# Nineteen reciprocal square roots: one GpSimd power in place of a guess and three Newton steps on VectorE

## The chip, the core and the metric

One NeuronCore of a Trainium2 chip runs one program. The metric is device microseconds of one execution, the median over several runs. Engines go by the profile's names: PE is TensorE, PEld its weight load, DVE VectorE, ACT ScalarE, POOL GpSimd, SP SyncE (it only issues DMAs here). Each engine works through its own list of instructions in order, and a semaphore is what makes one wait for another.

## The reference

Two stacked blocks on 256 tokens of width 1024, in float32. Block 1 normalises the embedding, modulates it by adaLN vectors, runs multi-head latent attention and RWKV7 side by side, a projection, a layer norm, a top-4 router and 32 experts. Block 2 has two layers of feed-forward, mixing (forgetting attention, dilated attention, HGRN2) and feed-forward, and a last norm. Each norm needs 1/sqrt of a few numbers per token:

```python
def layer_norm(x, g, b):
    xf = x.astype(jnp.float32)
    mu = xf.mean(-1, keepdims=True)
    var = jnp.square(xf - mu).mean(-1, keepdims=True)
    return ((xf - mu) * lax.rsqrt(var + LN_EPS) * g + b).astype(x.dtype)

def rms_norm(x, g):
    xf = x.astype(jnp.float32)
    return (xf * lax.rsqrt(jnp.square(xf).mean(-1, keepdims=True) + RMS_EPS) * g).astype(x.dtype)
```

The key of RWKV7 is divided by the norm of each head, and its output is normalised by head; these need the same function.

## The kernel before

The 256 tokens stand on 128 partitions in two halves, so a statistic per token is a tile of 128 x 1 or 128 x 2, and one per token and head of 128 x 8. The kernel is written as Python generators for the streams and is scheduled by a tile framework that simulates a timeline: it decides in which order each engine's list holds the instructions of independent streams. So an edit at one place can move others.

Line numbers here are those of the kernel before. The program in order of time:

- 0 to 262 us, block 1 up to the router. The embedding's norm (`ln_stats`, call at L551, two calls, 128 x 1) gives `xn` (L313), which PE transposes (L318) and L319 copies out as `axT`; `modT` (L591) comes from adaLN matrix-vector products on PE (`matvec`, weights `in_ada_w` against `cb`); L363 and L364 make the modulated input `moT` and its rounded copy, and then PE starts the input projection (L152, operands `w`). L1088 copies a constant, `iota`, which waits for the DMA of the constants `cst`. Attention and two halves `r` and `s` of RWKV7 then run interleaved. Calls: `rk` (L818, 128 x 8, once per half; its result is copied by L820 for a broadcast on PE), `mrs` (L628, 128 x 4), `gn` (L1033, 128 x 8, once per half, used by L1035), `mro` (L738, 128 x 2), `l2` (L563, 128 x 2, ahead of the router; `nb` at L565 follows it).
- 262 to 1231 us, the experts: 384 DMAs of 1 MB of weights.
- 1231 to 1252 us, `moe_end`: the second layer norm of block 1 (`l2` again). `block2_buffers` prepares the first weights of block 2 beside it, by splits of two-part float32 weights: ACT writes the high part (L198), and here POOL the low part (L203, four instructions of 128 x 1024; elsewhere DVE does L203).
- 1252 to 2309 us, block 2: triple matmuls of split operands (L152); `st` (L1538, 128 x 2, once per norm: four feed-forwards, two mixings, one final) and `hg` (L1865, 128 x 8, once per mixing). In a feed-forward and in mixing the norm's factor is wanted when the first products leave PSUM. ACT loads a table of functions whenever the next function is not in the one at hand (ACT_TABLE_LOAD).
- 2309 to 2329 us, `final`: the last norm, whose factor L1899 (DVE) and L1901 (ACT) apply to the output.

All 19 calls go through `rsqrt`, which issues 12 DVE instructions: an affine form or a floor (L179, L181), a bit trick on the integer view (L182), a multiplication by -0.5 (L183), and three Newton steps (L187 twice for n = 2, else L189 and L190, then L191).

Of the kernel before, what the change touches and what calls it, by code (L numbers as in the profile page):

```python
# [10 lines left out]
I32 = mybir.dt.int32  # L11
U32 = mybir.dt.uint32
AF = mybir.ActivationFunctionType
OP = mybir.AluOpType
# [13 lines left out]

BASE_AT, SETUP_AT, REST_AT = 6, 8, 10

PAD = (176, 8, 8, 8)
MAGIC = 12582912.0
PI_CLIP = 3.1415925
TWO_PI = (6.28125, 0.0019350051879882812, 3.0199159819471256e-07)
# [85 lines left out]
class K:  # L120
    def __init__(self, ctx, tc, I, dbg=None):
        self.ctx, self.tc, self.nc, self.I = ctx, tc, tc.nc, I
        self.dbg_ap = dbg or {}
        nc = self.nc
        self.per = ctx.enter_context(tc.tile_pool(name="per", bufs=1))
        self.rings = [ctx.enter_context(tc.tile_pool(name=n, bufs=b)) for n, b in (("ring", RING), ("ring2", RING2))]
        self.ring_i = None
        self.banks(ctx, p=2, r=2, s=2, m=2)
        self.n = 0
        self.plan = PLAN  # L130
        self.pairs = N_EXP // 2


    def t(self, pool, shape, tag, dt=F32, bufs=None):
        self.n += 1
        kw = {} if bufs is None else {"bufs": bufs}
        return pool.tile(shape, dt, tag=tag, name=f"{tag}_{self.n}", **kw)
# [33 lines left out]

    def rsqrt(self, pool, x, n, scale=1.0, eps=0.0, floor=None, tag="rs", eng=None):

        v = eng or self.nc.vector
        xe = self.t(pool, [128, n], tag + "x", bufs=2)
        y = self.t(pool, [128, n], tag + "y", bufs=2)
        u = self.t(pool, [128, n], tag + "u", bufs=2)
        if floor is None:
            v.tensor_scalar(xe, x, scale, eps, op0=OP.mult, op1=OP.add)  # L179
        else:  # L180
            v.tensor_scalar(xe, x, floor, None, op0=OP.max)  # L181
        v.tensor_scalar(y.bitcast(I32), xe.bitcast(I32), -0.5, 1597463007.0, op0=OP.mult, op1=OP.add)  # L182
        v.tensor_scalar(xe, xe, -0.5, None, op0=OP.mult)  # L183
        for _ in range(3):
            if n == 2:
                for c in (slice(0, 1), slice(1, 2)):
                    v.scalar_tensor_tensor(u[:, c], y[:, c], xe[:, c], y[:, c], op0=OP.mult, op1=OP.mult)  # L187
            else:
                v.tensor_tensor(u, y, y, op=OP.mult)  # L189
                v.tensor_tensor(u, u, xe, op=OP.mult)  # L190
            v.scalar_tensor_tensor(y, u, 1.5, y, op0=OP.add, op1=OP.mult)  # L191
        return y

    def split(self, hi, lo, src, hi_eng="s", lo_eng="v"):
# [33 lines left out]
    def load_consts(self):  # L228
        nc, I = self.nc, self.I
        n = C_ARR.shape[1]  # L230
        self.cst = self.t(self.A, [128, n + PAD[2]], "cst")[:, 0:n]
        first = self.t(self.per, [128, 129 + PAD[0]], "ident")[:, 0:129]
        nc.sync.dma_start(first, I["cst"][:, 0:129])
# [857 lines left out]
    def router(self, Ro, plg, mv, rs, space):  # L1091
# [46 lines left out]
        V.tensor_copy(self.over, most)  # L1138
        self.hgate = t(per, [128, 64 + PAD[1]], "hgate")[:, 0:64].rearrange("p (a e) -> p a e", a=2)
        V.tensor_scalar(self.hgate, gate, 0.5, None, op0=OP.mult)  # L1140
# [303 lines left out]
    def b2_setup(self, B):  # L1444
# [49 lines left out]
        for l in range(2):  # L1494
            nc.gpsimd.dma_start(self.ffw[:, l], I["w_in_2"][l, :, 768:772].rearrange("(k p) c -> p k c", p=128))
        self.rst2 = t(B, [128, T + PAD[3]], "rst2")[:, 0:T]
        nc.gpsimd.memset(self.rst2, 1.0)
# [451 lines left out]
```

## Time and profile before

| what | value |
|---|---|
| three runs | 2331.54, 2335.95, 2336.69 us, median 2335.95 |
| the profiled execution: time, span from first to last instruction | 2330.31 us, 2328.6 us |
| PE, PEld busy | 2264.0 us (97%), 1648.8 us (71%) |
| DVE busy | 1176.1 us (51%), 2237 instructions |
| ACT, POOL busy | 719.1 us (31%), 160.0 us (7%) |
| mean granted TensorE clock | 0.979 of full speed |

Busy shares are means over stages with different limits: the experts' stage follows the DMAs, block 2 follows PE, and the stage up to 262 us changes hands from one stretch to the next. A low share of DVE or POOL over the whole therefore does not say whether one of their instructions is waited for. That is read at each of the 19 places from the timeline, whose columns are start, length, engine and line, operation, and, in brackets, how long the engine was idle before and what released it.

### The profile page before, as it was taken

To read this page: it belongs to the slowest core of one execution; us is meant where nothing else is said; L and a number is where in the kernel's file an instruction comes from. 1 tells how busy PE (TensorE), PEld (TensorE's weight loads), DVE (VectorE), ACT (ScalarE), POOL (GpSimd) and SP (SyncE) were. 2 spreads that over 40 slices of the span, in tenths; PEclk is the share of its full clock that TensorE was granted. 3 is DMA by queue.
4 is the path that set the end of the run, shared out by engine and by line. 5 is a ranking of instruction groups with operands and counts; after the bars stand their busy time and mean duration, and the time that the engine had idled before them with its cause. 6 is when DMAs were issued, how large, how long until landed. Compare 5 with 4: busy or idle time off the path is not lost.

```text
span 2328.6 us, 37824 instructions
## 1 busy us (share of the span) xinstructions
PE 2264.0 (97%) x15957; PEld 1648.8 (71%) x15957; DVE 1176.1 (51%) x2237; ACT 719.1 (31%) x1187; POOL 160.0 (7%) x189
## 2 busy tenths in 40 slices
PE   7999999999999989999998999999999999999998
PEld 6777734444344433344436999989999999999998
DVE  5768322222142321222216666987657656997664
ACT  4333111001000110000004445654444445555443
POOL 3320000000000000000002001021001000121000
PEclk9889999999999999999998999999999999999999
DMA  8625999999999998999996555425555554535550
GB/s 325 188 75 188 339 409 404 411 412 412 419 415 420 420 420 348 412 407 411 410 414 245 187 184 168 156 76 181 181 181 181 182 182 148 180 107 180 182 182 19
DMA packets 275968, 626.47 MB, mean 269 GB/s; under 512 B 14576, under 2 KB 160368, under 8 KB 275760
## 3 DMA queue, kind: packets, MB, share of 16 engines
q1 hardware_dynamic: 274240, 621.38, 71.4%
q8 instruction: 128, 2.10, 0.4%
q0 software_dynamic: 1264, 2.08, 0.3%
q10 hardware_dynamic: 288, 0.52, 0.1%
q14 instruction: 48, 0.39, 0.0%
HBM read 622.89 MB, written 1.05 MB: 268 GB/s over the span
## 4 chain that ended last, share of the span: by engine, by line
PE 55%; DMA 3%; DVE 3%; issue 1%; ACT 1%; DVEq 0%; ACTq 0%
PE p L152 17%; PE s L152 17%; PE m L152 13%; PE r L152 8%; DMA w<-in_exp_w_dram 3%; DVE w L203 1%; PE r L1303 0%; PE s L1748 0%; DVE w L1510 0%; ACT w L1509 0%; PE r L1304 0%; DVE xx L1545 0%; DVE AT L1814 0%; DVE w L1804 0%; DVE z L1784 0%
## 5 line engine op out<-in xcount | busy, mean ns | idle before, releaser
L203 DVE TENSOR_TENSOR w<-w,w 128x1024 fp32r<-128x1024 f32 (+2 forms) x360 | 440.0, 1230 | 267.9 <-ACT w L198 267.8
L198 ACT CAST w<-w 128x1024 fp32r<-128x1024 f32 (+2 forms) x364 | 374.7, 1040 | 454.1 <-PE m L152 255.1
L152 PE MATMUL s<-w,w 128*128 128x256 f32 (+1 forms) x2392 | 306.3, 280 | 4.4 <-ACT w L198 4.4
L152 PE MATMUL m<-w,w 128*128 128x256 f32 (+1 forms) x2240 | 303.5, 285 | 3.7 <-DVE w L203 2.0
L152 PEld LDWEIGHTS s<-w,w 128*128 128x128 f32 (+1 forms) x2392 | 287.2, 189 | 6.7 <-ACT w L198 4.5
L152 PEld LDWEIGHTS m<-w,w 128*128 128x128 f32 (+1 forms) x2240 | 282.8, 192 | 6.9 <-DVE w L203 2.9
L152 PE MATMUL p<-w,xg 128*64 128x512 f32 x1024 | 269.3, 601 | 10.8 <-PEq L1365 5.6
L152 PE MATMUL s<-w,xg 128*64 128x512 f32 x1024 | 263.0, 597 | 0.0
L152 PE MATMUL p<-w,w 128*128 128x256 f32 x1728 | 228.8, 288 | 0.0
L152 PEld LDWEIGHTS p<-w,w 128*128 128x128 f32 x1728 | 214.5, 192 | 7.7 <-issue 6.0
L152 PEld LDWEIGHTS p<-w,xg 128*64 128x64 f32 x1024 | 89.9, 137 | 159.9 <-issue 135.8
L152 PEld LDWEIGHTS s<-w,xg 128*64 128x64 f32 x1024 | 90.0, 136 | 146.3 <-issue 134.3
L1207 DVE TENSOR_TENSOR ag<-r,adas 128x512 f32<-128x512 f32 x32 | 22.1, 692 | 306.7 <-PE r L1303 306.5
L1180 ACT ACTIVATE xg<-m,B,A 128x128 f32<-128x128 f32 x62 | 28.4, 457 | 364.4 <-DVE xg L1182 359.3
L152 PE MATMUL p<-w,u 128*64 128x512 f32 x512 | 126.8, 597 | 1.1 <-DMA w<-in_exp_w_dram 1.1
L152 PE MATMUL s<-w,u 128*64 128x512 f32 x512 | 121.9, 596 | 2.6 <-DMA w<-in_exp_w_dram 2.6
L1533 POOL TENSOR_TENSOR w<-w,th 128x256 f32<-128x256 f32 x47 | 40.8, 867 | 846.0 <-PE p L152 544.7
L152 PEld LDWEIGHTS s<-w,u 128*64 128x64 f32 x512 | 44.2, 136 | 73.4 <-issue 64.0
L152 PEld LDWEIGHTS p<-w,u 128*64 128x64 f32 x512 | 45.0, 136 | 70.2 <-issue 63.0
L1182 DVE TENSOR_SCALAR xg<-m,A,B 128x128 f32<-128x128 f32 x62 | 25.4, 410 | 136.8 <-PE m L152 126.9
L152 PEld LDWEIGHTS m<-oh,xx 128*128 128x128 f32 x496 | 59.1, 194 | 27.1 <-issue 24.3
L1299 ACT COPY h<-s 128x512 f32<-128x512 f32 x32 | 18.8, 586 | 192.7 <-PE s L152 192.7
(726 smaller groups left out, 2752.1 us busy)
## 6 DMA issues: line engine op xcount, KB each, us to landing
w<-in_exp_w_dram SPq DMA_DIRECT2D x384, 1024.0 KB, 18.1
w<-in_ffn_w_gate_dram SPq DMA_DIRECT2D x44, 1024.0 KB, 5.2
w<-in_ffn_w_up_dram SPq DMA_DIRECT2D x44, 1024.0 KB, 5.2
w<-in_ffn_w_down_dram SPq DMA_DIRECT2D x44, 1024.0 KB, 4.9
w<-in_w_in_dram SPq DMA_DIRECT2D x29, 1024.0 KB, 5.1
w<-in_ada_w_dram SPq DMA_DIRECT2D x24, 1024.0 KB, 5.5
w<-in_w_out_dram SPq DMA_DIRECT2D x8, 1024.0 KB, 4.9
w<-in_w_in_dram SPq DMA_DIRECT2D x8, 896.0 KB, 9.7
```

Of the source, the lines that this page charges most:

```text
L152: return self.nc.tensor.matmul(out, lhsT, rhs, start=start, stop=stop, skip_group_check=True, **kw)
L198: nc.scalar.copy(hi, src)
L203: (nc.vector if lo_eng == "v" else nc.gpsimd).tensor_tensor(lo, src, hi, op=OP.subtract)
L1180: S.activation(xg[:, d], p[:, j * 128:(j + 1) * 128], AF.Identity, scale=self.A2[:, d:d + 1], bias=self.B2[:, d:d + 1])
L1182: V.tensor_scalar(xg[:, d], p[:, j * 128:(j + 1) * 128], self.A2[:, d:d + 1], self.B2[:, d:d + 1], op0=OP.mult, op1=OP.add)
L1207: V.tensor_tensor(gl, pg, bg, op=OP.add)
L1299: S.copy(h[:, nb * 512:(nb + 1) * 512], hp[nb])
L1533: G.tensor_tensor(q[:, 0], q[:, 0], sq, op=OP.add)
```

## The change

`rsqrt` keeps its first DVE instruction (affine form or floor) and then issues one POOL instruction: the elementwise power of two tensors, with a tile `mhalf` of -0.5 as the exponent. `mhalf` (128 x 8) is set once by a POOL memset at the program's start, and a pad of the memory plan (`PAD`) is eight columns smaller for it. The scratch tile `u` is gone.

```diff
--- before.py
+++ after.py
@@ -28,7 +28,7 @@
 
 BASE_AT, SETUP_AT, REST_AT = 6, 8, 10
 
-PAD = (176, 8, 8, 8)
+PAD = (168, 8, 8, 8)
 MAGIC = 12582912.0
 PI_CLIP = 3.1415925
 TWO_PI = (6.28125, 0.0019350051879882812, 3.0199159819471256e-07)
@@ -127,6 +127,8 @@
         self.ring_i = None
         self.banks(ctx, p=2, r=2, s=2, m=2)
         self.n = 0
+        self.mhalf = self.t(self.per, [128, 8], "mhalf")
+        self.nc.gpsimd.memset(self.mhalf, -0.5)
         self.plan = PLAN
         self.pairs = N_EXP // 2
 
@@ -171,24 +173,14 @@
 
     def rsqrt(self, pool, x, n, scale=1.0, eps=0.0, floor=None, tag="rs", eng=None):
 
-        v = eng or self.nc.vector
+        V, G = self.nc.vector, self.nc.gpsimd
+        y = self.t(pool, [128, n], tag + "y", bufs=2)
         xe = self.t(pool, [128, n], tag + "x", bufs=2)
-        y = self.t(pool, [128, n], tag + "y", bufs=2)
-        u = self.t(pool, [128, n], tag + "u", bufs=2)
-        if floor is None:
-            v.tensor_scalar(xe, x, scale, eps, op0=OP.mult, op1=OP.add)
+        if floor is not None:
+            V.tensor_scalar(xe, x, floor, None, op0=OP.max)
         else:
-            v.tensor_scalar(xe, x, floor, None, op0=OP.max)
-        v.tensor_scalar(y.bitcast(I32), xe.bitcast(I32), -0.5, 1597463007.0, op0=OP.mult, op1=OP.add)
-        v.tensor_scalar(xe, xe, -0.5, None, op0=OP.mult)
-        for _ in range(3):
-            if n == 2:
-                for c in (slice(0, 1), slice(1, 2)):
-                    v.scalar_tensor_tensor(u[:, c], y[:, c], xe[:, c], y[:, c], op0=OP.mult, op1=OP.mult)
-            else:
-                v.tensor_tensor(u, y, y, op=OP.mult)
-                v.tensor_tensor(u, u, xe, op=OP.mult)
-            v.scalar_tensor_tensor(y, u, 1.5, y, op0=OP.add, op1=OP.mult)
+            V.tensor_scalar(xe, x, scale, eps, op0=OP.mult, op1=OP.add)
+        G.tensor_tensor(y, xe, self.mhalf[:, 0:n], op=OP.pow)
         return y
 
     def split(self, hi, lo, src, hi_eng="s", lo_eng="v"):
```

By count: DVE has 11 x 19 = 209 instructions fewer, POOL 19 powers and a memset more. The rows of the lists fall from 2073 to 1884 on DVE and rise from 171 to 191 on POOL. ACT's rise from 1074 to 1079: among them are four table loads, two in each mixing, since the two functions of `fox_masks` (L1694, L1695) now stand apart from L1760. In the rows below the lines of the changed kernel are lower by 8 than those of before (L195 is L203, L812 is L820).

DVE at the program's start, before: `lny` is the result of the embedding's norm, `w_80<-w_79` the normalised embedding, `modT` the adaLN vectors, `iota` the constant.

```order
L313 TENSOR_SCALAR w_80<-w_79,bmv_132,lny_135 128x1024
L191 SCALAR_TENSOR_TENSOR lny_156<-lnu_157,lny_156 128x1
L313 TENSOR_SCALAR w_80<-w_79,bmv_153,lny_156 128x1024
L319 COPY axT_70<-m_177 128x512
L319 COPY axT_70<-m_189 128x512
L591 TENSOR_TENSOR modT_128<-r_245,col_16_106 128x2x2
L357 TENSOR_SCALAR A_50_230<-modT_128 128x2
L358 TENSOR_TENSOR B_51_231<-col_16_106,A_50_230 128x2
L359 TENSOR_TENSOR B_51_231<-B_51_231,modT_128 128x2
L360 TENSOR_TENSOR A_50_230<-A_50_230,col_16_106 128x2
L1088 COPY iota_2687<-cst_88 128x96
L363 TENSOR_SCALAR moT_71<-axT_70,A_50_230,B_51_231 128x256 x2
```

DVE at the same place in the changed kernel:

```order
L295 SCALAR_TENSOR_TENSOR cact_126<-cth_124,col_17_108 128x8
L297 TENSOR_SCALAR cb_128<-cact_126 128x256
L583 TENSOR_TENSOR modT_130<-r_225,col_17_108 128x2x2
L349 TENSOR_SCALAR A_49_210<-modT_130 128x2
L350 TENSOR_TENSOR B_50_211<-col_17_108,A_49_210 128x2
L351 TENSOR_TENSOR B_50_211<-B_50_211,modT_130 128x2
L352 TENSOR_TENSOR A_49_210<-A_49_210,col_17_108 128x2
L1080 COPY iota_2623<-cst_90 128x96
L305 TENSOR_SCALAR w_82<-w_81,bmv_134,lny_136 128x1024
L305 TENSOR_SCALAR w_82<-w_81,bmv_144,lny_146 128x1024
L311 COPY axT_72<-m_157 128x512
L355 TENSOR_SCALAR moT_73<-axT_72,A_49_210,B_50_211 128x256 x2
```

The normalised embedding (L305, was L313) has moved from ahead of `modT` to behind the copy of `iota`, and the first `moT` stands between the two copies of `axT`.

DVE at the RWKV key norms, before, from the last steps of half `r` to the first of half `s`:

```order
L190 TENSOR_TENSOR rkru_948<-rkru_948,rkrx_946 128x8
L191 SCALAR_TENSOR_TENSOR rkry_947<-rkru_948,rkry_947 128x8
L820 COPY w_838<-rkry_947 128x512
L837 SCALAR_TENSOR_TENSOR w_895<-Z_72,col_37_195,w_894 128x256
L181 TENSOR_SCALAR rksx_922<-s_917 128x8
L837 SCALAR_TENSOR_TENSOR w_895<-Z_72,col_37_195,w_894 128x256
L182 TENSOR_SCALAR rksy_923<-rksx_922 128x8
L837 SCALAR_TENSOR_TENSOR w_838<-Z_72,col_37_195,w_837 128x256 x2
L183 TENSOR_SCALAR rksx_922<-rksx_922 128x8
L189 TENSOR_TENSOR rksu_924<-rksy_923 128x8
L190 TENSOR_TENSOR rksu_924<-rksu_924,rksx_922 128x8
L191 SCALAR_TENSOR_TENSOR rksy_923<-rksu_924,rksy_923 128x8
```

The same place in the changed kernel:

```order
L180 TENSOR_SCALAR rkrx_916<-r_910 128x8
L815 TENSOR_SCALAR w_874<-w_873,col_36_175,oka_204 128x256 x2
L834 COPY ebcs_936<-w_874 128x8
L815 TENSOR_SCALAR w_817<-w_816,col_36_175,oka_204 128x256 x2
L812 COPY w_818<-rkry_915 128x512
L180 TENSOR_SCALAR rksx_903<-s_897 128x8
L829 SCALAR_TENSOR_TENSOR w_875<-Z_74,col_36_175,w_874 128x256 x2
L829 SCALAR_TENSOR_TENSOR w_818<-Z_74,col_36_175,w_817 128x256 x2
L823 TENSOR_TENSOR w_817<-w_817,r_938 128x512
L825 TENSOR_TENSOR w_816<-w_817,w_816 128x512
L812 COPY w_875<-rksy_902 128x512
```

The two copies for the broadcast (L812, was L820) have no Newton steps ahead of them any more; that of half `s` stands behind four instructions of L829 and two of other lines.

POOL at the end of the experts, before: four low parts of weights, then the first products of block 2.

```order
L1909 MEMSET w_7768 128x1
L203 TENSOR_TENSOR w_7776<-w_7774,w_7776 128x1024
L203 TENSOR_TENSOR w_7779<-w_7774,w_7779 128x1024
L203 TENSOR_TENSOR w_7784<-w_7782,w_7784 128x1024
L203 TENSOR_TENSOR w_7787<-w_7782,w_7787 128x1024
L1533 TENSOR_TENSOR w_7768<-w_7768,th_7875 128x256
```

And in the changed kernel:

```order
L1901 MEMSET w_7671 128x1
L195 TENSOR_TENSOR w_7679<-w_7677,w_7679 128x1024
L195 TENSOR_TENSOR w_7682<-w_7677,w_7682 128x1024
L183 TENSOR_TENSOR l2y_7704<-l2x_7705,mhalf_67 128x2
L195 TENSOR_TENSOR w_7687<-w_7685,w_7687 128x1024
L195 TENSOR_TENSOR w_7690<-w_7685,w_7690 128x1024
L1525 TENSOR_TENSOR w_7671<-w_7671,th_7767 128x256
```

The power of `l2` stands behind the second low part and ahead of the third.

## Rows read from the trace of the kernel before

**Rows 1.** The page: busy us, share of the span and instructions by engine.

```profile
PE 2264.0 (97%) x15957; PEld 1648.8 (71%) x15957; DVE 1176.1 (51%) x2237; ACT 719.1 (31%) x1187; POOL 160.0 (7%) x189
```

**Rows 2.** Timeline, end of the MoE: start, length, engine line; idle, releaser.

```profile
1235.15 9.26 POOL L203 TENSOR_TENSOR w<-w,w 128x1024 fp32r<-128x1024 f32 x4 [25.72 <-ACT w L198]
...
1239.87 2.26 DVE L182 TENSOR_SCALAR l2y<-l2x 128x2 int32<-128x2 int32 x1
...
1246.20 0.16 DVE L565 SCALAR_TENSOR_TENSOR nb<-bmv,l2y 128x2 f32<-128x2 f32 x1
...
1247.34 0.69 PE L1421 MATMUL p<-ident,w 128*128 128x128 f32 x2 [8.73 <-DVE w L1416]
```

**Rows 3.** Timeline, final norm.

```profile
2320.26 0.16 DVE L179 TENSOR_SCALAR stx<-s 128x2 f32<-128x2 f32 x1 [1.79 <-PE s L152]
...
2322.41 0.16 DVE L191 SCALAR_TENSOR_TENSOR sty<-stu,sty 128x2 f32<-128x2 f32 x1
...
2322.66 0.69 ACT L1901 ACTIVATE w<-p,sty 128x512 f32<-128x512 f32 x1 [3.75 <-DVE sty L191]
```

**Rows 4.** Timeline, router's norm.

```profile
261.45 0.17 DVE L179 TENSOR_SCALAR l2x<-bmv 128x2 f32<-128x2 f32 x1
...
263.82 0.16 DVE L191 SCALAR_TENSOR_TENSOR l2y<-l2u,l2y 128x2 f32<-128x2 f32 x1
```

**Rows 5.** Windows: length, busy (count) by engine, PEclk, DMA share, GB/s.

```profile
95.00:100.00 5.00, 2.14 (x22) 1.62 (x24) 4.83 (x15) 0.79 (x2) 1.43 (x2) 0.84 0.59 184
100.00:135.00 35.00, 35.00 (x448) 26.68 (x442) 20.43 (x52) 4.99 (x11) 8.08 (x6) 0.50 0.29 96
225.00:230.00 5.00, 5.00 (x46) 2.60 (x46) 4.71 (x28) 1.77 (x4) 0.45 (x1) 0.69 0.87 315
260.00:265.00 5.00, 2.54 (x19) 2.26 (x18) 4.75 (x30) 1.54 (x4) 0.00 (x0) 0.72 1.02 419
```

**Rows 6.** Timeline, RWKV key norms: DVE, then PE.

```profile
92.25 0.43 DVE L820 COPY w<-rkry 128x512 f32<-128x512 f32 x1
...
100.68 0.40 DVE L820 COPY w<-rksy 128x512 f32<-128x512 f32 x1
...
99.20 1.94 PE L152 MATMUL p<-w,cb 128*32 128x256 f32 x16 [2.86 <-DVE modT L603]
```

**Rows 7.** ACT group of table loads at L1768; windows of mixing, layer 1.

```profile
L1768 ACT ACT_TABLE_LOAD x2 | 2.6, 1283 | 0.0
...
1475.00:1560.00 85.00, 84.91 (x701) 81.42 (x700) 82.87 (x141) 51.23 (x88) 17.97 (x11) 1.00 0.38 124
1565.00:1570.00 5.00, 3.11 (x20) 2.16 (x18) 3.72 (x24) 2.82 (x10) 0.00 (x0) 0.95 0.00 0
```

**Rows 8.** Groups on POOL, one on DVE: shape, count | busy us, mean ns.

```profile
L878 POOL TENSOR_TENSOR w<-w,cst 128x512 f32<-128x512 f32 x8 | 10.6, 1341 | 32.3 <-PE s L152 15.9 <-ACT w L861 14.3 <-PE r L152 2.0
...
L203 POOL TENSOR_TENSOR w<-w,w 128x1024 fp32r<-128x1024 f32 x4 | 9.3, 2350 | 25.7 <-ACT w L198 25.7
...
L1909 POOL MEMSET w<- 128x1 f32 x5 | 0.5, 99 | 196.8 <-PE p L152 192.4 <-DMA w<-in_exp_w_dram 4.1 <-issue 0.3
...
L203 DVE TENSOR_TENSOR w<-w,w 128x1024 fp32r<-128x1024 f32 x342 | 421.5, 1239 | 252.5 <-ACT w L198 252.3
```

**Rows 9.** Instructions of L191: count, min/median/max ns, first and last start.

```profile
L191 DVE SCALAR_TENSOR_TENSOR mrsy<-mrsu,mrsy x3: 144/155/1237, 115.5 to 122.4; 128x4 f32<-128x4 f32 x3
```

**Rows 10.** Timeline, start: DVE, then PE.

```profile
11.03 0.81 DVE L313 TENSOR_SCALAR w<-w,bmv,lny 128x1024 f32<-128x1024 f32 x1
13.41 1.35 DVE L319 COPY axT<-m 128x512 f32<-128x512 f32 x2 [1.57 <-PE m L318]
...
19.01 0.21 DVE L1088 COPY iota<-cst 128x96 f32<-128x96 f32 x1 [1.29 <-DMA cst<-in_cst_dram]
...
21.20 0.80 PE L152 MATMUL s<-w,w 128*128 128x256 f32 x2 [4.42 <-ACT w L198]
21.93 1.94 PE L152 MATMUL r<-w,cb 128*32 128x256 f32 x16
```

## The prediction

> **What bounds the kernel now.** I read the page first: PE is busy 97% of the span and DVE 51%, in 2237 instructions [rows 1]. So 209 DVE instructions are worth nothing by their number; what counts is where PE, or a stage's end, waits for a norm's factor. I then took the 19 calls one by one in the timeline and the windows and looked for what stood idle. Four places show a wait that the Newton chain ends, and the reader should see each in its rows: the layer norm at the end of the experts, where PE is idle 8.73 us [rows 2]; the last norm, where ACT is idle 3.75 us until L191 [rows 3]; the router's norm, where the chain runs from 261.45 to 263.98 us [rows 4] in a window with PE busy 2.54 of 5 us [rows 5]; and the RWKV key norms, where PE waits 2.86 us for an instruction (L603) queued on DVE among the Newton steps [rows 6]. In the other calls the factor is used late and PE has matmuls to run: in mixing PE is busy 84.91 of 85 us though DVE is at 82.87 [rows 7].
>
> **The price of a power.** No row shows one. From below it is the smallest POOL instruction, a memset of 128x1, 0.10 us; from above a two-input instruction of 128x1024 at 2.35 us, the middle being 128x512 at 1.34 us [rows 8]. The tiles have 1 to 8 columns, which lies near the lower end, but a power is more work than a product. I take 0.5 us, and 0.1 us for each hand-over from DVE to POOL and back, an estimate from ACT, which starts 0.09 us after DVE's L191 has ended [rows 3].
>
> **End of the experts.** POOL runs four low parts from 1235.15 for 9.26 us, 2.315 each, so the second ends at 1239.78 and the fourth at 1244.41. DVE's L182 begins at 1239.87, just behind the third, and takes 2.26 us for a tile of 128x2: it ends when that part ends. L183 and the steps follow, and `nb` at 1246.20 [rows 2]. In the new order the power stands behind the second low part: it begins at about 1239.95, just when its input is there, and ends at 1240.45. Next on DVE is `nb` (two SBUF inputs), and on POOL the third low part, which begins first, since it needs no hand-over. I expect `nb` to be held as L182 was: L191, the same kind of instruction, took 1237 ns once against a median of 155 [rows 9]. So `nb` ends when that low part does, 1240.45 + 2.35 = 1242.8, against 1246.36: 3.5 us earlier, and PE's transposes with it (0.98 us behind it, as now). If `nb` slips in ahead, the gain is 5.5; with a power of 2.35 us and `nb` held it is 1.7; with 0.1 us and not held 5.9.
>
> The Trainium skill, page "SBUF — State Buffer", section "Who interferes with whom", says that a DVE instruction with two SBUF inputs contends with a GpSimd instruction that reads SBUF, and that the later one is blocked for the whole of the earlier. By it this place gives 3.5 us, without it 5.5; the trace agrees (2.26 us for L182, 1237 ns for L191).
>
> **Last norm.** From the end of L179 (2320.42) to ACT's start (2322.66) are 2.24 us [rows 3]; a power with its hand-overs is 0.7. Gain 1.5; with 0.1 us 1.9; with 2.35 us a loss of 0.3. Nothing else uses POOL there.
>
> **Router's norm.** 261.62 to 263.98 us, 2.36 us, all in sequence on DVE and nothing else for `nb` to wait for [rows 4]. Gain 2.36 - 0.7 = 1.6, bounds 2.0 and -0.2. This stands ahead of the experts, whose weights stream in a chain of DMAs; I count it in full, since the first weights are used only behind the router.
>
> **RWKV key norms.** L820 of half `r` runs at 92.25 and of half `s` at 100.68 [rows 6]. In the new order no Newton step stands ahead of them. The six that stood directly ahead of half `r`'s took some 2.0 us by L191's durations, five at 0.155 and one held for 1.24 [rows 9]; the eleven of half `s` are worth 1.7, and 1.1 more where POOL holds one: 4.8 in all. So L603, on DVE behind most of them, moves up by about 5 us, and the 2.86 us of idle PE ahead of 99.20 go. Bounds: 0, if PE then waits for the next thing, and 5 if what follows moves with it.
>
> **Per-head norm and attention norm (212 to 227 us).** Three calls less are 33 DVE instructions of 0.155 us [rows 9], 5.1 us of a DVE that is 4.71 of 5 us busy in 225 to 230; but PE is busy 5.00 of 5 us there [rows 5]. PE's work stays, at a granted clock of 0.69 that a shorter wait ahead may lift. I take 1.5; bounds 0 and 5.1.
>
> **Start: a loss.** The power itself is hidden, but the order moves. Before, the normalised embedding (L313) is done at 11.84, its copies `axT` at 14.76, and PE starts the projection at 21.20, 2.2 us behind `iota`, which waits until 19.01 for the DMA of its constants [rows 10]. In the new order L305 stands behind that copy on DVE: from 19.2 the two L305 take 1.62 us; from the start of the second to the end of `axT` are 14.76 - 11.03 = 3.73 us, so `axT` is there at 23.7, and with the 2.1 us that follow `iota` now the projection starts at 25.8, 4.6 us late. In the meantime PE can do matrix-vector products that now stand behind the first matmuls (1.94 us at 21.93 [rows 10], and more like it later), so the loss is 1.6 to 4.6; I take 2.5. No wait of DVE is longer than now; what queues behind `iota` is the whole input path.
>
> **Mixing and feed-forward.** Eleven DVE instructions less per call, with PE full: 0. Against it stand two more table loads of 1.28 us on ACT in each mixing [rows 7]; ACT is busy 51.23 of 85 us there, so they are hidden: 0, and 5.1 us for both layers if they are not. At `hg` PE has 1.89 us idle in 1565 to 1570, which the attention streams cause as much: 0, at most -1.9 per layer.
>
> **Sum.** 2.5 - 2.9 - 1.5 - 1.6 - 3.5 - 1.5 = -8.5 us. The profiled execution took 2330.31, which gives 2321.8. The runs shown are 2331.54, 2335.95 and 2336.69, so the profiled one lies 5.6 us under the median; with it the four have a mean of 2333.6, and I forecast 2325.
>
> **Rivals.** (1) *The clock stays up.* From 100 to 135 us PE works at a granted clock of 0.50, the lower of its two levels (1.2 GHz), after 95 to 100, in which it was busy only 2.14 of 5 us [rows 5]. If the key norms come 5 us sooner, that gap may be too small for the clock to fall. 35 us of full PE work would shrink towards half, a further 14 us or so, since part of it waits for chains on DVE: 2311. For it speaks that the gap is just what the change shortens, against it that other waits fill part of it. (2) *The first 262 us give nothing.* The projection starts 4.6 late and the gains at the key norms and per-head norms are lost in PE's own list: 4.6 - 1.6 - 3.5 - 1.5 = -2.0: 2331, no change that can be told. (3) *The power is slow, and the kernel slower.* About six calls stand in sequence with something that waits (two key norms, the two layer norms, the last norm, a per-head norm). Beyond 0.5 us each microsecond of a power costs 6 us: the gain is gone at 0.5 + 8.5/6 = 1.9 us, and at 3.4 us the time is 2325 + 17 = 2342. Against it speaks that a product of 512 columns takes 1.34 us, and ours has 8. (4) *The table loads are not hidden:* -8.5 + 5.1 = -3.4: 2330.
>
> The Trainium skill's page "GPSIMD Engine Reference", section "Engine selection", speaks against the change: elementwise work belongs on VectorE, GpSimd being about 2x slower with two inputs. The trace agrees for large tiles (L203 takes 2.35 us on POOL and 1.24 on DVE [rows 8]), but here one instruction stands for eleven; by that factor a power would be 0.155 x 2 = 0.3 us, an estimate that changes the sum by about 1 us.
>
> **How the numbers follow.** Forecast 0.45, rival 1 0.15, rival 2 0.18, rival 3 0.10, rival 4 0.12. The measurement tells from no change about 0.2%, 4.7 us. Faster: nearly all of the forecast and rival 1, a third of rival 4, a little of rival 2: 0.67. Slower: most of rival 3 and the edges of 2 and 4: 0.11. Same: 0.22. The range leaves out the far halves of rivals 1 and 3: 2308 to 2336; the forecast's own is 2317 to 2331.
>
> **What would show it.** POOL rows of 0.3 to 0.8 us for the powers; `nb` at the end of the experts of over 2 us, and PE's transposes about 3.5 us closer to the last expert's matmul; ACT's last idle time near 2.3 us; the projection's first matmul near 25; the key norms' copies about 5 us apart at most, and the granted clock in the 35 us behind them. The prediction is wrong if a power takes over 1.5 us, if the clock there is above 0.8, or if PE in mixing waits for ACT behind a table load.

## The result, and the profile after

The changed kernel takes 2311.2 us (median of four runs, 2308.78 to 2316.36) against 2334.95 us before (four runs): a ratio of 0.989, with an interval of 0.9869 to 0.9912. It is 1.1% faster, clear of the noise, and the time lies within the range given, but 13.8 us under the forecast of 2325. The profiled execution took 2310.61 us, with a span of 2308.8 us. The terms of the sum are compared below on the two profiled executions, which differ by 19.7 us.

The page's first part, beside [rows 1]:

```profile
PE 2247.2 (97%) x15957; PEld 1630.4 (71%) x15957; DVE 1151.7 (50%) x2028; ACT 723.9 (31%) x1191; POOL 175.9 (8%) x209
```

PE executes the same 15957 matmuls and is busy 16.8 us less. That is most of the gain, and it is not what one expects when a wait of PE is taken away: a wait that goes leaves the busy time as it was. By stage it is 14.0 us less in the feed-forwards and 4.6 less ahead of the router, where the granted clock is higher (0.95 in place of 0.90), and 2.1 more in the experts.

The powers among the groups on POOL (count | busy us, mean ns of one | idle time before, and what ended it):

```profile
L183 POOL TENSOR_TENSOR sty<-stx,mhalf 128x2 f32<-128x2 f32 x7 | 4.9, 701 | 13.6 <-DVE stx L182 13.6
L183 POOL TENSOR_TENSOR hgy<-hgx,mhalf 128x8 f32<-128x8 f32 x2 | 3.3, 1640 | 50.2 <-DVE hgx L182 50.2
...
L183 POOL TENSOR_TENSOR lny<-lnx,mhalf 128x1 f32<-128x1 f32 x2 | 1.1, 580 | 0.1
L183 POOL TENSOR_TENSOR mrsy<-mrsx,mhalf 128x4 f32<-128x4 f32 x1 | 1.1, 1058 | 0.0
```

A power of 1, 2, 4 and 8 columns takes 0.58, 0.70, 1.06 and 1.64 us: about 0.43 us and 0.15 us for each column. The two at the key norms, also of 8 columns, take 1.71 and 1.83 us.

Where the 19.7 us went, read from the starts of the same instructions in both timelines (the affine step that opens each call, and `nb`):

| stretch | before, us | after, us | difference | forecast |
|---|---|---|---|---|
| start to the router's `l2x` | 261.45 | 255.49 | -6.0 | -1.9 |
| router's norm, `l2x` to `nb` | 2.56 | 1.01 | -1.6 | -1.6 |
| experts, `nb` to `l2x` | 975.62 | 977.39 | +1.8 | 0 |
| end of the experts, `l2x` to the first `stx` | 21.95 | 18.35 | -3.6 | -3.5 |
| four feed-forwards | 762.82 | 749.85 | -13.0 | 0 |
| two mixings | 295.86 | 299.90 | +4.0 | 0 |
| last norm, `stx` to the end | 8.29 | 6.85 | -1.4 | -1.5 |

The three places at which the chain ended a wait came out as forecast. Whether the router's 1.6 us reach the end is another matter: from its `l2x` to the next one the pair shows 978.2 and 978.4 us. In the three kernels with Newton steps there it is 977.6 to 978.2 us, in the seven with a power and the weights' slots in their old place 974.3 to 978.4, 976.1 in the mean. So the gain is likely, but this pair does not show it. The end of the experts, beside [rows 2], in the timeline of after:

```profile
1233.89 0.20 DVE L182 TENSOR_SCALAR l2x<-bmv 128x2 f32<-128x2 f32 x1
...
1234.17 0.71 POOL L183 TENSOR_TENSOR l2y<-l2x,mhalf 128x2 f32<-128x2 f32 x1
1234.87 4.63 POOL L195 TENSOR_TENSOR w<-w,w 128x1024 fp32r<-128x1024 f32 x2
1234.92 2.30 DVE L557 SCALAR_TENSOR_TENSOR nb<-bmv,l2y 128x2 f32<-128x2 f32 x1 [0.82 <-POOL l2y L183]
1237.14 0.80 DVE L1408 TENSOR_SCALAR w<-r,bmv,l2y 128x512 f32<-128x512 f32 x1
...
1238.00 0.69 PE L1413 MATMUL p<-ident,w 128*128 128x128 f32 x2 [5.12 <-DVE w L1408]
```

The next low part (L195) starts 0.05 us ahead of `nb`, and `nb`, an instruction of two columns, ends with the first of the two at 1237.2. PE is idle 5.12 us ahead of its transposes where it was 8.73 us.

The last norm, beside [rows 3]: ACT waits 2.32 us in place of 3.75 us.

```profile
2301.99 0.16 DVE L182 TENSOR_SCALAR stx<-s 128x2 f32<-128x2 f32 x1 [1.79 <-PE s L154]
2302.23 0.70 POOL L183 TENSOR_TENSOR sty<-stx,mhalf 128x2 f32<-128x2 f32 x1 [2.94 <-DVE stx L182]
2302.96 0.69 ACT L1893 ACTIVATE w<-p,sty 128x512 f32<-128x512 f32 x1 [2.32 <-POOL sty L183]
```

The start, beside [rows 10], DVE and PE:

```profile
19.21 0.21 DVE L1080 COPY iota<-cst 128x96 f32<-128x96 f32 x1 [0.83 <-DMA cst<-in_cst_dram]
19.34 1.53 DVE L305 TENSOR_SCALAR w<-w,bmv,lny 128x1024 f32<-128x1024 f32 x2
...
26.38 0.51 PE L154 MATMUL s<-w,w 128*128 128x256 f32 x2
```

The projection starts 5.2 us later than before, as the new order made one expect. But the first half's key norm opens at 83.82 us, against 83.77 us before: the loss is gone by then.

The key norms, beside [rows 6], DVE:

```profile
83.82 0.14 DVE L180 TENSOR_SCALAR rkrx<-r 128x8 f32<-128x8 f32 x1
...
88.27 1.50 DVE L812 COPY w<-rkry 128x512 f32<-128x512 f32 x1 [0.53 <-POOL rkry L183]
...
95.64 1.48 DVE L812 COPY w<-rksy 128x512 f32<-128x512 f32 x1
```

The copies come 4.0 and 5.0 us earlier. `modT`, for which PE waited before, hardly moves: L603 is L595 now, and comes 0.4 us earlier. Before and after (DVE):

```profile
99.00 0.15 DVE L603 TENSOR_TENSOR modT<-p,col 128x2 f32<-128x2 f32 x1
...
98.58 0.14 DVE L595 TENSOR_TENSOR modT<-p,col 128x2 f32<-128x2 f32 x1
```

It stands behind both copies, each of which now takes 1.5 us, on a DVE that is never idle from 95 to 100 us. PE's wait there is not gone, it has another cause (PE in the same window):

```profile
97.17 1.16 PE L154 MATMUL s<-ident,w 128*128 128x128 f32 x8 [2.25 <-DVE w L812]
```

The windows, beside [rows 5]:

```profile
90.00:95.00 5.00, 4.92 (x42) 4.21 (x42) 4.03 (x6) 1.16 (x3) 5.00 (x4) 1.00 0.86 292
95.00:100.00 5.00, 2.83 (x44) 2.82 (x46) 5.00 (x10) 0.00 (x0) 1.83 (x2) 0.93 0.82 289
100.00:135.00 35.00, 33.89 (x763) 25.77 (x759) 26.31 (x52) 7.73 (x16) 17.68 (x17) 0.86 0.27 93
...
105.00:110.00 5.00, 3.89 (x56) 3.72 (x56) 4.93 (x9) 0.37 (x1) 3.96 (x4) 0.61 0.91 344
...
115.00:135.00 20.00, 20.00 (x505) 15.12 (x503) 13.30 (x28) 5.50 (x10) 8.57 (x11) 1.00 0.17 56
```

From 100 to 135 us the granted clock is 0.86 in place of 0.50, and 763 matmuls are done there in place of 448. The clock falls here too (0.93, 0.61), but it is back at 1.00 from 115 us on.

That leaves the 13 us of the feed-forwards. A matmul has a stationary operand, here the weights, and a moving one that is streamed past it, here the activations. Twelve matmuls of the same shape, before and after, PE in one feed-forward each (runs of 12 follow each other without idle time, so the distance of two starts is the time of 12). Before:

```profile
1356.95 1.60 PE L152 MATMUL m<-w,w 128*128 128x256 f32 x12
1358.39 1.60 PE L152 MATMUL p<-hg,w 128*128 128x256 f32 x12
1359.83 1.60 PE L152 MATMUL r<-hg,w 128*128 128x256 f32 x12
```

After:

```profile
1298.28 1.52 PE L154 MATMUL r<-hg,w 128*128 128x256 f32 x12
1299.64 1.52 PE L154 MATMUL p<-hg,w 128*128 128x256 f32 x12
1301.00 1.52 PE L154 MATMUL r<-hg,w 128*128 128x256 f32 x12
1302.36 1.58 PE L154 MATMUL s<-w,w 128*128 128x256 f32 x12
1303.78 1.60 PE L154 MATMUL m<-w,w 128*128 128x256 f32 x12
```

Before, 12 matmuls take 1.44 us whatever their operand. After, those with `hg` as the moving operand take 1.36 us (the first of a group 1.38), those with `w` still 1.44 (the first behind such a group 1.42). The trace has 2112 products of `hg`, `hq` or `z` with weights, all in the four feed-forwards: 176 runs of 12 at 0.08 us are 14 us, the size of the gain. These tiles lie behind the scratch tile `u` of `st`. `u` is gone, so they stand 64 bytes lower; the weights, the stationary operand, stay where they were. By the addresses of the built program the distance from stationary to moving operand, modulo 512 bytes, was 0 for all of them and is now 448. The traces hold no addresses; what they show is the time.

### The profile page after: what moved, and what is told of

The parts are those of the page before. It is cut to its first block, busy times and chain, and to the rows that moved or that the text cites. A ratio compares the mean times of both kernels' runs of the same rounds, so it can differ in the third digit from the quotient of the medians.

```text
span 2308.8 us, 37622 instructions
## 1 busy us (share of the span) xinstructions
PE 2247.2 (97%) x15957; PEld 1630.4 (71%) x15957; DVE 1151.7 (50%) x2028; ACT 723.9 (31%) x1191; POOL 175.9 (8%) x209
## 4 chain that ended last, share of the span: by engine, by line
PE 49%; DVE 6%; DMA 3%; issue 2%; ACT 1%; POOL 0%; POOLq 0%; DVEq 0%; ACTq 0%
PE s L154 16%; PE p L154 13%; PE m L154 13%; PE r L154 6%; DMA w<-in_exp_w_dram 3%; DVE w L195 2%; DVE AT L1806 1%; DVE w L1800 0%; DVE w L1796 0%; DVE ate L1733 0%; DVE w L1502 0%; PE r L1295 0%; ACT w L190 0%; DVE z L1776 0%; POOL w L195 0%
## 5 line engine op out<-in xcount | busy, mean ns | idle before, releaser
L195 DVE TENSOR_TENSOR w<-w,w 128x1024 fp32r<-128x1024 f32 (+2 forms) x360 | 437.7, 1224 | 260.0 <-ACT w L190 258.0
```

Of the source, the lines that this page charges most:

```text
L195: (nc.vector if lo_eng == "v" else nc.gpsimd).tensor_tensor(lo, src, hi, op=OP.subtract)
```

## Experiments

Two theories stand against each other. P, the place: most of the gain comes from tiles that lie 64 bytes lower. R, the square roots: it comes from the chains, their order and the clock. Each ratio is to the kernel before on the same chip. Lengths of a stage are from one profiled execution, and `ffn` and `mix` are the times from one `stx` to the next.

**Places alone, in the kernel before (b_shift64).**

```diff
-PAD = (176, 8, 8, 8)
+PAD = (176, 8, 8, 24)
```

> The kernel before, Newton steps and all, with nothing changed but 16 more columns of padding in one tile of block 2's pool, so that every tile behind it (th, R, hq, hg, z and so on) lies 64 bytes higher; the order on all engines stays the same. Theory P (place): the faster feed-forwards of the changed kernel come from where hq, hg and z lie against the weights, not from rsqrt. Then matmuls of hg, hq, z against weights take 0.1133 us each instead of 0.1200 (a run of 12 in 1.36 us instead of 1.44); 2120 of them give 14 us, so a time some 14 us under the kernel before. Rival D (DVE time freed by the removed Newton steps lets PE run closer): the time is that of the kernel before within 3 us.

Ratio 0.9996 (0.9967 to 1.0025): no change. The runs with `hg` take 1.41 us in place of 1.44 and the four feed-forwards 758.3 us, 4.5 less. So a move of 64 bytes upward is not worth 14 us, and P in the form "any move" falls.

**The changed kernel with those tiles back at their old place (a_back64).** The order of instructions is unchanged.

```diff
-PAD = (168, 8, 8, 8)
+PAD = (168, 8, 8, 24)
```

> The changed kernel with 16 more columns of padding in the same tile, so that hq, hg and z lie again at the addresses that they had before; the order on all engines stays that of the changed kernel. Theory P: 14 us slower than the changed kernel, near 2325, runs of 12 back at 1.44 us. Rival D: the changed kernel's time within 3 us.

Ratio 0.9953 (0.9929 to 0.9977). The feed-forwards are back at 762.9 us, and so are the runs (PE):

```profile
1301.15 1.60 PE L154 MATMUL r<-hg,w 128*128 128x256 f32 x12
1302.59 1.60 PE L154 MATMUL s<-w,w 128*128 128x256 f32 x12
```

What is left, 0.47% or 11 us (5.4 to 16.6), is the square roots' part.

**The kernel before with those tiles 64 bytes lower (b_place448).** The Newton steps and the order stay; `u` of `st` shares the allocation of `x`.

```diff
+if tag == "st":
+    xu = self.t(pool, [128, 2 * n], tag + "x", bufs=2)
+    xe, u = xu[:, 0:n], xu[:, n:2 * n]
# ...
```

> The kernel before with its rsqrt as it was, in the same order on all engines; only the scratch tile u of the st calls now lies in the same allocation as x, so that hq, hg and z lie 64 bytes lower, where the changed kernel has them. Theory P (what counts for a matmul of split operands is how far the moving operand lies from the weights, modulo 512 bytes: 0 gives 1.44 us for 12, +64 gives 1.41, -64 gives 1.36): runs of 12 with hg, hq, z at 1.36 to 1.38 us, each feed-forward as long as in the changed kernel (186.6, 188.8, 189.7, 184.8 us between the st calls), 13 us under the kernel before. Rival (it takes the removed Newton steps as well as the place): feed-forwards as before, 190.1 us, no change in time.

Ratio 0.9937 (0.9917 to 0.9957), 14.7 us without a square root touched. The feed-forwards take 749.8 us, as after, and the two mixings 292.8, 3.1 less than before, though none of the 2112 products is in them. PE, where `hq` takes over from `w`:

```profile
1357.42 1.52 PE L152 MATMUL r<-hq,w 128*128 128x256 f32 x12
1358.78 1.52 PE L152 MATMUL p<-hq,w 128*128 128x256 f32 x12
1360.14 1.52 PE L152 MATMUL r<-hq,w 128*128 128x256 f32 x12
1361.50 1.58 PE L152 MATMUL s<-w,w 128*128 128x256 f32 x12
```

0.9937 x 0.9953 = 0.989: the two parts together are the whole. So both directions show that the place of these tiles is worth some 14 us, with Newton steps and without.

**Is it the distance, and would the products of other operands gain too? (a_ringgap, a_stride32, a_stride64, a_fixed448).** All four are the changed kernel with other places for the weights' slots: a gap between the two rings of slots; slots 32 and 64 bytes further apart; the five fixed input slots in a ring of their own, 448 bytes off.

```diff
# a_ringgap
-PAD = (168, 8, 8, 8)
+PAD = (168, 8, 8, 40)
# ...
+self.gap = gap.tile([128, 16], F32, tag="gap", name="gap_0")   # between the two rings
# a_stride32
-return self.t(self.rings[which], [128, 2048], "w")
+return self.t(self.rings[which], [128, 2056], "w")[:, 0:2048]
# a_stride64
-PAD = (168, 8, 8, 8)
+PAD = (24, 8, 8, 8)
-return self.t(self.rings[which], [128, 2048], "w")
+return self.t(self.rings[which], [128, 2064], "w")[:, 0:2048]
# a_fixed448
-PAD = (168, 8, 8, 8)
+PAD = (168, 8, 8, 24)
# ...
+self.gap = gap.tile([128, 112], F32, tag="gap", name="gap_0")  # between ring2 and ring3
-self.fixed = [self.slot_tile(1) for _ in range(5)]
+self.fixed = [self.slot_tile(2) for _ in range(5)]
```

> The changed kernel with a gap of 64 bytes between the two rings of weight slots, so that the second ring (with the split inputs xhi and xlo, and some weights) lies at 64 bytes past a multiple of 8192 and the first at a multiple; hq, hg, z lie at 128 past a multiple of 1024. If what counts is that both operands of a matmul lie at the same remainder, matmuls of xhi, xlo against weights from the first ring become as fast as those of hg (0.1133 us), the others stay at 0.1200: 8 to 25 us under the changed kernel. If what counts is the place of hg alone, the time of the changed kernel or some us above it.

> The changed kernel with 32 bytes more between two weight slots (8224 instead of 8192), so that the split inputs xhi, xlo and the weights mostly lie at different remainders of 512 bytes; the order stays. Theory P in its general form: the 6342 products of xhi or xlo that now lie at distance 0 from their weights leave 1.44 us for 12 too; were all of them at 1.36, 6342 x 6.7 ns = 42 us would go, and with distances of mixed value 15 to 40 us go: 2270 to 2300 us. Rival (only the tiles hg, hq, z gain, for another reason than the distance): the changed kernel's time or somewhat above it.

> The changed kernel with 64 bytes more between two weight slots and a smaller pad ahead of them, so that the products of xhi and xlo stand at the distances 0, 192, 256, 320, 384 and 448 modulo 512 in turn. Theory P: runs of 12 at 1.44 us only where the distance is 0, at 1.36 to 1.38 where it is 448, near 1.41 where it is 192 or 256 as in the run with 32 bytes; it shows what 320 and 384 do. 2290 to 2320 us in all. Rival: the time of 12 does not follow the distance of its operands.

> The changed kernel with the five slots that hold the split inputs of block 2 (xhi, xlo among them) in a ring of their own, 448 bytes past the other slots, so that 5568 more of the products of split operands have their moving operand at -64 bytes (448 modulo 512) from the weights; some of block 1 is scheduled in another order for it. Theory P: these products go from 1.44 us for 12 to 1.36 to 1.38 like those of hg, hq and z; 5568 x 5 to 6.7 ns = 28 to 37 us less than the changed kernel, ratio to the kernel before near 0.974. Rival (what gains is peculiar to hg, hq, z): runs of xhi stay at 1.44 us, the changed kernel's time.

| kernel | ratio | interval | four ffn, us | 12 matmuls, us |
|---|---|---|---|---|
| a_ringgap | 0.9982 | 0.9958 to 1.0007 | 758.6 | `w` 1.44 (distance still 0), `hg` 1.41 |
| a_stride32 | 0.9945 | 0.9923 to 0.9968 | 752.0 | 1.40 to 1.44 |
| a_stride64 | 0.9931 | 0.9911 to 0.9951 | 749.1 | 1.36 to 1.45 by the distance |
| a_fixed448 | 0.9941 | 0.992 to 0.9962 | 742.8 | 1.41 in three ffn, 1.36 in the last |

None beats the changed kernel. Part of the reason is a stage that the table does not show: from the router's `nb` to the next `l2x` the three kernels with moved slots (a_ringgap, a_stride32, a_stride64) take 984.1, 986.7 and 982.2 us, where the ten kernels with the slots in their old place take 973.3 to 977.4. So the place to which the experts' weights are loaded matters as well; no run shows why. In a_stride64 the distances are mixed, and by the built program's addresses the runs sort by them: 0 gives 1.43 to 1.45 us, 448 gives 1.36 to 1.38, 64 and 320 give 1.36 to 1.42, 384 gives 1.42 to 1.43, 192 and 256 give 1.41 to 1.44. Distance 0 is the slowest wherever distances are mixed. But the distance alone doesn't set the rest: a_fixed448 has the weights' products at 448 as well, and PE shows 12 of them at 1.42 us in one feed-forward

```profile
1360.91 1.58 PE L159 MATMUL s<-w,w 128*128 128x256 f32 x12
1362.33 1.58 PE L159 MATMUL m<-w,w 128*128 128x256 f32 x12
```

and at 1.36 us in the last:

```profile
2202.30 1.52 PE L159 MATMUL s<-w,w 128*128 128x256 f32 x12
2203.66 1.52 PE L159 MATMUL m<-w,w 128*128 128x256 f32 x12
```

So in a_fixed448 the last feed-forward falls to 178.7 us (184.8 after), while its order in block 1 was another one and its router's `l2x` came at 275.7 us. What else enters stays open.

**Single calls back to Newton steps (a_newton_start, a_newton_rk, a_newton_hg, a_pow_ends).** The changed kernel with the old `rsqrt` for some tags.

```diff
+if tag in NEWTON:
+    return self.rsqrt_newton(pool, x, n, scale, eps, floor, tag)
# a_newton_start: NEWTON = ("ln",)      a_newton_rk: ("rkr", "rks")      a_newton_hg: ("hg",)
# a_pow_ends: ("ln", "mrs", "rkr", "rks", "gnr", "gns", "mro", "hg")
# ...
```

> The changed kernel with the guess and the Newton steps kept for the two calls of the embedding's norm alone, so that the normalised embedding stands again ahead of the copy of iota on DVE; the other 17 calls are powers; hq, hg, z stay where the changed kernel has them. Theory (the order costs 5 us at the start): the projection's first matmul near 21.3 instead of 26.4 us, the router's norm 3 to 5 us sooner, the whole 3 to 5 us faster than the changed kernel, about 2307. Rival (the weights' DMAs or the matrix-vector products set the pace of the first 50 us): the router's norm within 1.5 us, the time the same.

Ratio 0.994 (0.9912 to 0.9968), not better than 0.989. PE starts the projection 5.0 us sooner than after, and nothing of it arrives at the key norms (`rkrx` at 84.23 us). So nothing shows that the new order at the start costs time; the two intervals touch at 0.9912, and the kernel with the old order may even be the slower one. Its profiled execution, 2309.21 us, is the fastest of ten (median 2317.08) and cannot show why. PE:

```profile
21.35 0.80 PE L155 MATMUL s<-w,w 128*128 128x256 f32 x2 [4.54 <-ACT w L215]
```

> The changed kernel with the guess and the Newton steps kept for the two RWKV key norms alone. Theory C (the key norms' Newton chain makes the gap on PE after which the clock falls): PE is again idle some 5 us in 90 to 100 us, the granted clock of 100 to 135 us is 0.50 to 0.60 instead of 0.67 to 0.88, the router's norm begins 4 to 8 us later than the changed kernel's 255.5. Rival (the gain of the first 262 us comes from the per-head and attention norms instead): the router's norm within 2 us of it and the clock above 0.65.

Ratio 0.9899 (0.9864 to 0.9934), which can't be told from after. PE is busy 5.14 of 10 us in 90 to 100 (7.75 after) and the granted clock from 100 to 135 is 0.64, between 0.50 and 0.86. So PE is idle there as it was before (busy 5.07 of 10 us), and yet the clock is not back at 0.50. On time it decides nothing.

> The changed kernel with the guess and the Newton steps kept for the two hg calls in mixing alone, where a power of 8 columns takes 1.64 us. Theory M (mixing is 2 us longer in each layer because of the order that came with the powers and two more table loads, not of the power itself): mixing as long as in the changed kernel, 149 to 150 us between its st call and the next, the time the same within 2 us. Rival (the power at hg is what is waited for): mixing 147.9 us as before, 4 us faster in all.

Ratio 0.9897 (0.9862 to 0.9932); mixing stays at 148.9 and 150.0 us. The power at `hg` is not what lengthens mixing.

> The changed kernel with powers only at the l2 and st calls (two columns, 0.70 us each); the guess and the Newton steps are kept at ln, mrs, rk, gn, mro and hg; hq, hg, z stay where the changed kernel has them. Theory (the gains are the place of the tiles, 13 us, the layer norm at the experts' end, 3.6, the last norm, 1.4, and some 6 in the first 262 us that come from the calls now put back): 2 to 6 us slower than the changed kernel, the granted clock at 0.50 in 100 to 135 us, the router's norm at 260 us or later, mixing at 147.5 us. Rival (the calls of the first 262 us give nothing lasting): the changed kernel's time or under it.

Ratio 0.9927 (0.9905 to 0.9948): 3.7 parts in a thousand above after, with intervals that overlap a little. The window that [rows 5] show for before:

```profile
100.00:135.00 35.00, 35.00 (x448) 26.49 (x442) 20.66 (x52) 4.77 (x10) 8.08 (x6) 0.50 0.29 98
```

The clock is back at 0.50, with the same 448 matmuls, and `l2x` comes at 271.4 us. So the clock follows from the calls of block 1, with the order that comes with them.

Which of them it is can be looked for in the mean granted clock over the whole span, which is on record for every execution and not for the profiled one alone:

| kernels | executions | median |
|---|---|---|
| Newton steps in block 1 up to the router's norm (before on each chip, b_shift64, b_place448, a_pow_ends) | 7 to 31 each | 0.975 to 0.979 |
| powers in all of block 1, its order as after (seven kernels) | 4 to 10 each, 53 in all | 0.983 to 0.986 |
| a_newton_rk, Newton steps at the key norms alone | 6 | 0.983 |
| a_newton_start, Newton steps at the embedding's norm alone | 10 | 0.980 |
| a_fixed448, all powers, another order in block 1 | 12 | 0.979 |

The key norms' Newton steps leave the clock where the powers have it; those of the embedding's norm, or another order alone, take most of the difference away. No run shows why the start of the program weighs so much.

**The held `nb` (a_no_nb).** At the end of the experts all four halves go to DVE, which needs no `nb`.

```diff
-S.activation(xn[:, a, 512:], self.acc2[a][1], AF.Identity, scale=rs[:, a:a + 1], bias=nb[:, a:a + 1])
+V.tensor_scalar(xn[:, a, 512:], self.acc2[a][1], mv[:, a, 0:1], rs[:, a:a + 1], op0=OP.subtract, op1=OP.mult)
# ...
```

> The changed kernel without nb at the end of the experts: all four halves of the layer norm are now made by DVE from PSUM (subtract the mean, times the factor), so DVE has nothing with two SBUF inputs between l2x and them; the order of PE, POOL and SP stays. Theory H (nb is held for 2.30 us by POOL's third low part, and that is why the place gained 3.6 us and not 5.5): the first of the four starts within 0.1 us of the power's end, at 1.0 us behind l2x instead of 3.25, PE's transposes start 2 us sooner, and from l2x to the next st call pass 16.2 to 17.0 us instead of 18.3; 1.4 to 2 us in the whole, which the times can hardly tell. Rival (DVE is late for another reason, a semaphore or POOL itself): the first of the four starts some 3 us behind l2x as now, and nothing is gained.

Ratio 0.9887 (0.9859 to 0.9915), the same as after within the interval. At the place itself, in the timeline:

```profile
1236.02 0.21 DVE L182 TENSOR_SCALAR l2x<-bmv 128x2 f32<-128x2 f32 x1
1236.31 0.71 POOL L183 TENSOR_TENSOR l2y<-l2x,mhalf 128x2 f32<-128x2 f32 x1
1237.01 4.65 POOL L195 TENSOR_TENSOR w<-w,w 128x1024 fp32r<-128x1024 f32 x2
1237.05 0.81 DVE L1409 TENSOR_SCALAR w<-r,bmv,l2y 128x512 f32<-128x512 f32 x1 [0.82 <-POOL l2y L183]
```

An instruction with a PSUM input starts 0.04 us behind the same low part and isn't held: 0.81 us. From `l2x` to the first `stx` are 16.48 us in place of 18.35. Without the hold, and with two halves moved from ACT to DVE, the place is 1.9 us shorter, which a measurement of the whole can't tell.

## Why the prediction was right, and where it was wrong

- **End of the experts, last norm, router's norm: right.** -3.6, -1.4 and -1.6 us against -3.5, -1.5 and -1.6. The hold of `nb` was forecast and is shown by a_no_nb. The Trainium skill's page "SBUF — State Buffer", section "Who interferes with whom", on which the prediction draws, agrees with both: two SBUF inputs are held (2.30 us), one from PSUM is not (0.81 us). But L182, which the prediction gives as a case of that rule, has only one input in SBUF. The rows show that such instructions are held too: 2.26 us at L182 [rows 2].
- **The price of a power: right within its bounds, too low for eight columns.** 0.5 us was taken; two columns take 0.70 and eight take 1.64 to 1.83, over the 1.5 us that were named as a sign of being wrong. It did no harm to the sum, because the places that count have two columns. At the key norms POOL also had a queue: `rkrx` is there at 83.96 us and its power starts at 86.52, behind two other instructions (POOL, after):

```profile
86.52 1.71 POOL L183 TENSOR_TENSOR rkry<-rkrx,mhalf 128x8 f32<-128x8 f32 x1
```

  So the copies moved up 4.0 and 5.0 us and not more. Rival 3 falls: it needed 1.9 us at each of six calls. The estimate of 0.3 us by the Trainium skill's page "GPSIMD Engine Reference", section "Engine selection", was two to six times too low.
- **Start, +2.5: mis-sized, 0 or less.** The projection came 5.2 us late (4.6 forecast), but the key norms do not wait for it. The step that failed is "the loss is 1.6 to 4.6": PE's own lag there is not on the path to 83.8 us, and a_newton_start gains nothing by taking it away. By the clocks above, the powers at the start may even be part of the gain.
- **Key norms and per-head norms, -4.4: too small, and the wait did not go.** The step that failed is "L603 moves up by about 5 us": it moved 0.4, and PE waits 2.25 us at 97.17 in place of 2.86. The pair of profiles gives -6.0 for the whole stretch to the router, +2.5 included in the forecast -1.9. One execution says little here: the three kernels in the order of before had `l2x` at 261.5, 268.4 and 277.6 us, a_pow_ends at 271.4. The seven with all powers of block 1 and its unchanged code (after, a_back64, a_ringgap, a_stride32, a_stride64, a_newton_hg, a_no_nb) had it at 255.5 to 265.7. The means are 269.7 and 261.3, so some 8 us, an estimate. With it goes the clock: 0.50 to 0.52 in the first four, 0.66 to 0.88 in the seven. So rival 1's higher clock came, and with 0.86 it passed the 0.8 that was named as a sign against the forecast; the rival's 14 us are not reached. Its reason is not borne out: the clock did fall behind the key norms and came back sooner, and a_newton_rk has the old wait of PE without the old clock. Nor does the time of the whole follow the clock of this stretch: a_newton_start, with 0.73 there, and a_pow_ends, with 0.50, have ratios of 0.994 and 0.9927. What keeps the clock up stays open.
- **Mixing and feed-forward, 0: the step that failed.** The prediction counted eleven DVE instructions less on a full PE and looked at ACT's table loads, but put no cost on the scratch tile `u` that goes, the one edit that moves operands of the bound engine. It gave -13.0 us in the feed-forwards, more than the whole forecast. Shown by a_back64 (gone) and b_place448 (there without a power).
- **Rival 4, mixing.** With equal places, mixing is longer with the powers: 150.0 and 150.0 us after against 146.4 and 146.4 in b_place448, and at the old places 148.9 and 149.7 in a_back64 against 147.9 and 148.0. So 3 to 7 us for both layers, around the rival's 5.1, and forecast as 0. PE's own waits don't name ACT. The view of waits, PE in mixing of layer 1, after (us in total, times, longest):

```profile
PE r L154 <- DVE w L1818: 1.1, 1, 1.1
PE s L1740 <- DVE ate L1733: 0.8, 1, 0.8
PE m L154 <- DVE w L195: 0.6, 1, 0.6
PE r L154 <- DVE w L1800: 0.6, 1, 0.6
PE r L154 <- DVE AT L1806: 0.4, 1, 0.4
```

  They are 3.5 us, against 2.6 before (1.9 for L1741, 0.7 for L203). In the two layers together PE is idle for 8.5 us, against 4.8 in b_place448: about half of the 7 us. Three of them, on DVE's L1818, L1800 and L1806, are new. Four more table loads and another order of mixing came together with the powers of `st`, and no run parts the two: which of them it is stays open.

The time of rival 1, 2311, was hit by another sum: 14.7 us from the tiles' place, a term that stood in no case, and 11 us (5.4 to 16.6) from the square roots, of which the prediction had 8.5. By stages the 11 are some -6.6 at the three ends, some -8 in block 1, and 3 to 7 lost in mixing. That the time lies in the range is in part luck: with the tiles left at their place the change takes 2324.35 us (a_back64), against 2332.72 before on the same chip, which is the forecast, and there too the misses in block 1 and in mixing offset each other.

## What to carry to other kernels

An edit that frees or resizes a tile moves every tile behind it: compare the addresses of PE's operands before and after, and time the move by itself, with a pad that undoes it, before crediting the edit. A chain of small operations off the full engine's path is worth what waits at its end, so a single instruction on a slower engine paid at the three places where another engine waited, and at the key norms its queue counted more than its own time. Where a stage's length differs by 16 us between executions of one order, take its gain from several kernels and not from one pair of profiles, and compare what is on record for every execution, such as the mean granted clock.

## What the runs showed of the hardware

- Twelve matmuls of 128x256 with the same shapes and the full clock take 1.44, 1.41 or 1.36 us by where the moving and the stationary operand lie. By the built program's addresses a distance of 0 modulo 512 bytes gave 1.43 to 1.45 us in all kernels (1.42 right behind a faster group); 448 gave 1.36 to 1.38 except in part of a_fixed448. The rule behind it is not found.
- A GpSimd power costs 0.58, 0.70, 1.06 and 1.64 to 1.83 us for 1, 2, 4 and 8 columns of 128 partitions.
- A DVE copy of 128x512 with a broadcast source (L812) took 1.50 and 1.48 us beside POOL's two-input instructions, 0.43 and 0.40 without them before [rows 6]: part of what the shorter chain gave went into that.
- With the slots for streamed weights moved by 32 or 64 bytes, the experts' stage took 982.2 to 986.7 us in three kernels, against 973.3 to 977.4 in ten. No run shows the reason.
